# Lead ups by VectorE's lag, rows at an even pace, a selection put off and an earlier fetch of V, in a decoder layer on one core

## The chip, the cores and the metric

The kernel runs on one core of one Trainium2 chip. The metric is the time of the device in microseconds, of which the median over several runs is taken. TensorE (PE in the rows) does the matrix products, VectorE (DVE) elementwise work, searches and the gathered rows, ScalarE (ACT) activations and the emptying of PSUM, GpSimd (POOL) the indirect DMAs, SyncE (SP) the plain DMAs.

## The reference

One layer over 512 tokens of width 1024, float32. The cut below keeps what is computed.

```python
h = layer_norm(x, ln_emb_g, ln_emb_b)
rq, rk, rv, rg, fq, fk, fv, ff, gr, gf = jnp.split(h @ w_in[i], split_points, axis=-1)
y_ret = (silu(rg) * group_norm_heads(retention(rotary(rq), rotary(rk), rv))) @ w_ret_o[i]
y_fox = forgetting_attention(fq, fk, fv, log_sigmoid(ff + b_forget[i])) @ w_fox_o[i]
merged = sigmoid(gr + b0) * y_ret + sigmoid(gf + b1) * y_fox
h = layer_norm(ALPHA * h + merged @ w_out[i], ln1_g[i], ln1_b[i])
ple = sigmoid(h @ w_ple_gate[i] + b_ple_gate[i]) * (p[i] @ w_ple[i])
ch = peer(h, w_peer_q[i], peer_sub_keys[i], peer_u[i], peer_v[i]) + ple
h = layer_norm(ALPHA * h + ch, ln2_g[i], ln2_b[i])

def peer(x, ...):      # per token: 8 heads, 16 of 128*128 experts each
    sc = einsum(x @ w_q, sub_keys)            # two halves of 128 keys
    s, idx = top_k(sc, 16)                    # per half
    top_s, pos = top_k(all 256 sums, 16)      # the selection
    eid, gate = ids at pos, softmax(top_s)
    act = gelu(einsum(expert_u[eid], x)) * gate
    return einsum(act, expert_v[eid])
```

## The kernel before

The 512 tokens are four blocks of 128. Blocks 0 and 1 (`FIRST`) go ahead, blocks 2 and 3 (`REST`) follow, and the two pairs treat the experts differently.

For `FIRST`, each of the 128 (8 heads by 16) chosen experts of a token is fetched: one **row** is an indirect DMA on POOL (L1023) that brings 128 expert vectors, one for each token, 0.524 MB, and one VectorE instruction, either a product with the token summed (`row<-row,xg`, L1029, an up row, 256 of them) or an update of the sum (`h<-row,ghid,h`, L1039, a down row, 256). Eight buffers hold rows. For `REST` all 16384 experts are computed: 128 **banks** of 128 experts. The **up** of a bank is 8 matmuls of `h1f` with `ur` (a load of 1 MB holds two banks) into PSUM `hid` (two buffers), followed by a GELU on ScalarE into `a`. The down is 12 matmuls with V split in high and low parts (`vh`, `vl`). Between them the activation is multiplied with a dense gate `gw`, made by the **spread**.

The stages, by the profiled run: up to 24 us tokens are loaded, normalised and transposed; up to 300 `first_blocks` (projections and attention of `FIRST`); up to 410 `product_keys` of block 0 and of block 1, each by itself, and half of the embedding gate; up to 462 keys and values of `REST` (`keys_values`) and the start of its retention; up to 760 `last_blocks` (attention of `REST`, `w_out`, the norm, the other half of that gate); up to 906 `channel` begins with `product_keys` of `REST`, its embedding gate, in which `select` of block 2 runs; up to 1022 the spread of block 2, with `select` of block 3 beside it; up to 1130 the spread of block 3; up to 1182 remaining ups and the first loads of the dense loop; up to 1781 the dense loop over the banks; then the last norm and the output.

`lead` is 46: so many ups are done ahead of the dense loop (**lead ups**), and RES = 4 more into the accumulator's PSUM. A **spread** transposes the three routing tiles of a block (`gt`, copied by ScalarE to `gtr`), then makes, for each 8 tokens, two one-hot masks on VectorE (`oa`, `ob`), scales `oa` by the gate on ScalarE, multiplies the two on TensorE (`gp`) and copies the result on ScalarE to `stg` (two buffers). After each 32 tokens the full `stg` (2 MB) is written from ScalarE's queue to `gd` in DRAM, eight times in all; the dense loop reads it back as `gw`.

What sets the order: VectorE, POOL and TensorE run the instructions in the order in which the program emits them, from the product keys of `FIRST` on; a scheduler sets the order of ScalarE and SP. A `Feed` is a list of pieces of work with a rate; `tick()`, called after each group of a projection and each step of a spread, takes pieces: from `k.later`, from `k.side` (selections, norms), from `k.fill` (products of the embedding, later lead ups), then rows. Rows come from `k.feed` whenever `Clock.row()` allows. `Clock` adds up planned times of TensorE (`pe`), VectorE (`dve`) and the DMA (`dma`); a row is allowed when VectorE's plan, with this row, is not past TensorE's. Helper calls all record line L188 (L194 in the changed kernel).

Of the kernel before, what the change touches and what calls it, by code (L numbers as in the profile page):

```python
# [131 lines left out]
class Clock:  # L132
# [4 lines left out]
    def __init__(self):  # L137
        self.pe = self.dve = self.dma = 0.0
        self.before = None
# [23 lines left out]
    def row(self):  # L163

        if self.dve + self.ROW > self.pe or self.dma > self.pe + 5:
            return False
        self.dve = max(self.dve, self.pe - 12) + self.ROW
        self.dma = max(self.dma, self.pe - 5) + self.ROW
        return True
# [33 lines left out]
def setup(ctx, tc, I):  # L203
# [9 lines left out]
    k.feed, k.side, k.fill = Feed(), Feed(), Feed()  # L213
# [12 lines left out]
    def tick():  # L226
        due, k.later = k.later, []
        for f, *a in due:
            f(*a)
        k.side()  # L230
        k.fill()
        rows()
# [364 lines left out]
def attention(k, G, act, rq):  # L597
# [21 lines left out]
    side.drain()  # L619
    yf = slot([P, nt, 512], F32, "H4", k.uniq("yf"))  # L620
# [45 lines left out]
def first_blocks(k, unsplit):  # L666
# [4 lines left out]
    tokens_load(k, G)  # L671
    for t in G.blocks:
        tokens_norm(k, t)
        transpose_block(k, k.h0[:, t, :], act, t, 8)
# [15 lines left out]
    k.side.rate = k.fill.rate = 0.5  # L690
    k.fill.items = embeddings(k)
# [3 lines left out]
    k.fill.drain()  # L695
# [17 lines left out]
def last_blocks(k, act, rq, h10):  # L713
# [7 lines left out]
    k.h1 = k.slot([P, 8, G.N], F32, "S3", "h1f")  # L721
    for u, t in enumerate(G.blocks):
        layer_norm(k, k.h0[:, t, :], k.h0[:, t, :], g1, b1, st=sts[u], share=False)
# [47 lines left out]
def embeddings(k):  # L771
# [16 lines left out]
    return [(products, g, t) for g in range(2) for t in range(NT)]  # L788
# [104 lines left out]
def spread(k, sp, routed, n0, gd):  # L893
# [6 lines left out]
    nc.scalar.activation(tr, ps, AF.Copy)  # L900
    sh = [P, 8, P]
# [32 lines left out]
class Experts:  # L934


    def __init__(self, k, dense, gd, lead, ap, ph):
        self.k, self.gd, self.lead, self.ap, self.ph = k, gd, lead, ap, ph
        self.nd, self.ND = len(dense), len(dense) * P
        self.act, self.vw, self.gw = {}, {}, {}  # L940
# [14 lines left out]
    def load(self, b, dv):  # L955
        k, nc = self.k, self.k.nc
        if b % 2 == 0:
            self.vraw = dv.tile([P, 2, D], F32, tag="vraw", name=k.uniq("vr"))
            nc.sync.dma_start(self.vraw, k.I["vP"][b // 2])
        hi = dv.tile([P, D], F32R, tag="vhi", bufs=3, name=k.uniq("vh"))  # L960
        lo = dv.tile([P, D], F32R, tag="vlo", bufs=3, name=k.uniq("vl"))
        nc.scalar.activation(hi, self.vraw[:, b % 2], AF.Copy)
        self.vw[b] = (hi, lo, self.vraw[:, b % 2])
# [78 lines left out]
def channel(k, dense, lead, ctx):  # L1042
# [5 lines left out]
    ex = Experts(k, dense, gd, lead, ap, ph)  # L1048
    with ExitStack() as c1:
        k.pp = c1.enter_context(tc.tile_pool(name="pp2", bufs=4, space=PSUM))  # L1050
        k.px = c1.enter_context(tc.tile_pool(name="px2", bufs=2, space=PSUM))
        rp = c1.enter_context(tc.tile_pool(name="rp", bufs=2))
        routed = [[rp.tile([P, HEADS * K], F32, bufs=1, name=f"rt{n}_{i}") for i in range(3)] for n in range(2)]
        with ExitStack() as c2:
# [31 lines left out]
    nc.sync.dma_start(g2, bcast(I["ln2_g"], D))  # L1086
    nc.sync.dma_start(b2, bcast(I["ln2_b"], D))
# [7 lines left out]
    for b in range(2):  # L1095
        ex.load(b, dp)
# [4 lines left out]
    for b in range(3):  # L1101
        ex.gate(b, dp)
    for b in range(2):
        ex.remainder(*ex.act[b])
    done = lead + RES
    for b in range(NK):
        if b + 2 < NK:
            ex.load(b + 2, dp)
# [31 lines left out]
def decoder_layer(ctx, tc, I, lead):  # L1140
# [4 lines left out]
    with ExitStack() as c1:  # L1145
# [25 lines left out]
        k.side.rate = 1.25  # L1171
        k.clock.meet()
        for u, t in enumerate(FIRST.blocks):
# [3 lines left out]
            k.side.items += [g.route(rp, s16[:, 0], i16[:, 0]), (g.rows,)]  # L1177
        k.side.items += [(c2.close,)]
# [9 lines left out]
        last_blocks(k, act, rq, h1)  # L1188
    channel(k, list(REST.blocks), lead, ctx)
# [28 lines left out]
```

## Time and profile before

| | |
|---|---|
| median of three runs | 1838.2 us (1829.74 to 1840.3) |
| profiled execution, own time | 1832.67 us |
| its span | 1830.9 us |
| granted TensorE clock over the span | 0.964 |
| busy: TensorE, VectorE, ScalarE, POOL | 91%, 75%, 34%, 35% of the span |
| bytes moved by DMA | 566.51 MB, 309 GB/s over the span |

A row of a timeline gives the start, the duration, the engine, the line, the operation, what it writes and reads, and in brackets how long its engine had been idle and what ended that. One fp32 matmul leaves two records, so an up of 8 matmuls is x16. A table by stretch gives the busy time of each engine in it, the granted clock, the share of time in which the DMA engines were busy and what they moved.

### The profile page before, as it was taken

The page shows a single profiled execution, that of the slowest core. Times are in us where ns is not written, and L with a number is a line of the kernel's source. Part 1 is how long each engine was busy: PE and PEld are TensorE (multiplying, and loading weights), DVE is VectorE, ACT ScalarE, POOL GpSimd, SP SyncE. Part 2 cuts the span into 40 slices and gives each one's busy share as a digit, 9 for nine tenths or more (in the row PEclk, how much of TensorE's full clock was granted, in tenths as well). Part 3 has the DMA queues.
Part 4 walks back from the last instruction along what each step waited for, and adds up shares of the span by engine and source line. Part 5 has one row for each costly group of instructions (what it writes and reads, how often), then busy time and mean ns, then how long its engine had stood idle before and what let it go on. Part 6 is the DMA issues. An engine that isn't in the chain of part 4 may idle for free.

```text
span 1830.9 us, 23147 instructions
## 1 busy us (share of the span) xinstructions
PE 1666.7 (91%) x8224; PEld 1370.6 (75%) x8224; DVE 1375.3 (75%) x2624; ACT 614.6 (34%) x1160; POOL 648.9 (35%) x523
## 2 busy tenths in 40 slices
PE   5999999997899998899488989799999999999996
PEld 4898998873757885486377878588888887888785
DVE  6544364799778878889978775487878877887887
ACT  4445643212023320111355654233323333333332
POOL 1000000014567765432107352243434444544440
PEclk9999999999999999999789989899999999999998
DMA  7543455778899999995349999899999999999992
GB/s 264 167 138 127 146 163 191 249 237 323 309 341 403 409 409 407 364 376 204 124 132 369 305 398 312 314 408 383 389 391 406 402 371 373 410 408 393 402 367 91
DMA packets 171684, 566.51 MB, mean 309 GB/s; under 512 B 18352, under 2 KB 51632, under 8 KB 155184
## 3 DMA queue, kind: packets, MB, share of 16 engines
q1 hardware_dynamic: 64944, 279.78, 40.8%
q0 software_dynamic: 73728, 268.47, 37.9%
q10 hardware_dynamic: 32896, 16.78, 3.1%
q8 instruction: 65, 1.06, 0.2%
q14 instruction: 51, 0.42, 0.1%
HBM read 543.99 MB, written 20.97 MB: 309 GB/s over the span
## 4 chain that ended last, share of the span: by engine, by line
PE 47%; issue 20%; DVE 16%; DMA 14%; ACT 2%; POOL 1%; SPq 0%; DVEq 0%; POOLq 0%; ACTq 0%
PE hid L188 19%; PE acc L188 18%; PE pj L188 6%; DMA gd<-stg 5%; DMA row<-in_peer_v,geu 4%; DMA row<-in_peer_u,geu 3%; DVE h L1039 2%; PE gp L188 2%; DVE s L188 2%; DVE i L188 2%; DVE row L1029 1%; DVE w L188 1%; DVE pos L188 1%; DMA wr<-in_w_peer_q 1%; PE lg L188 1%
## 5 line engine op out<-in xcount | busy, mean ns | idle before, releaser
L1023 POOL DMA_INDIRECT row<-in_peer_v,geu x256 | 323.4, 1263 | 428.5 <-DVE h L1039 374.5
L1023 POOL DMA_INDIRECT row<-in_peer_u,geu x256 | 313.9, 1226 | 409.1 <-DVE row L1029 231.7
L188 PE MATMUL hid<-h1f,ur 128*128 128x256 f32 x1984 | 451.6, 381 | 3.1 <-DMA ur<-in_uT 2.6
L188 PEld LDWEIGHTS hid<-h1f,ur 128*128 128x128 f32 x1984 | 376.5, 191 | 57.2 <-issue 3.9
L1039 DVE SCALAR_TENSOR_TENSOR h<-row,ghid,h 128x1024 f32<-128x1024 f32 x256 | 327.5, 1279 | 22.1 <-DMA row<-in_peer_v,geu 19.4
L1029 DVE SCALAR_TENSOR_TENSOR row<-row,xg 128x1024 f32<-128x1024 f32 x256 | 306.8, 1217 | 19.4 <-DMA row<-in_peer_u,geu 18.9
L188 DVE TENSOR_TENSOR vl<-vr,vh 128x1024 fp32r<-128x1024 f32 x128 | 156.8, 1226 | 133.9 <-ACT vh L188 116.1
L188 PE MATMUL acc<-vh,ah 128*128 128x512 f32 x512 | 214.9, 420 | 0.0
L188 PE MATMUL acc<-vh,al 128*128 128x512 f32 x512 | 201.8, 394 | 11.8 <-DVE al L188 11.8
L188 PE MATMUL acc<-vl,ah 128*128 128x512 f32 x512 | 201.0, 393 | 4.8 <-DVE vl L188 4.8
L188 DVE TENSOR_TENSOR wl<-wr,wh 128x1024 fp32r<-128x1024 f32 x72 | 90.5, 1257 | 92.7 <-ACT wh L188 92.5
L188 ACT ACTIVATE vh<-vr 128x1024 fp32r<-128x1024 f32 x128 | 130.4, 1050 | 41.0 <-PE acc L188 27.0
L188 PE MATMUL pj<-h1f,wr 128*128 128x128 f32 (+1 forms) x768 | 124.0, 322 | 16.9 <-DMA wr<-in_w_peer_q 11.3
L188 ACT ACTIVATE a<-hid 128x256 f32<-128x256 f32 x124 | 47.1, 382 | 254.3 <-PE hid L188 254.3
L188 PEld LDWEIGHTS pj<-h1f,wr 128*128 128x128 f32 x768 | 111.7, 198 | 27.8 <-DMA wr<-in_w_peer_q 10.4
L188 PEld LDWEIGHTS acc<-vh,al 128*128 128x128 f32 x512 | 96.6, 189 | 35.9 <-DVE al L188 15.7
L188 ACT ACTIVATE ah<-a 128x256 fp32r<-128x256 f32 x128 | 53.1, 416 | 199.3 <-DVE a L188 178.2
L188 PE MATMUL pj<-hT,wr 128*128 128x256 f32 x512 | 117.6, 385 | 0.7 <-DMA wr<-in_w_in 0.7
L188 PEld LDWEIGHTS acc<-vl,ah 128*128 128x128 f32 x512 | 96.8, 189 | 26.4 <-DVE vl L188 5.5
L285 POOL TENSOR_TENSOR h<-h,b 128x512 f32<-128x512 f32 x6 | 9.7, 1619 | 294.9 <-ACT h L188 294.9
L188 PEld LDWEIGHTS acc<-vh,ah 128*128 128x128 f32 x512 | 96.7, 189 | 19.1
L188 PEld LDWEIGHTS pj<-hT,wr 128*128 128x128 f32 x512 | 97.4, 193 | 15.0 <-DMA wr<-in_w_in 1.1
(225 smaller groups left out, 2506.0 us busy)
## 6 DMA issues: line engine op xcount, KB each, us to landing
ur<-in_uT SPq DMA_DIRECT2D x64, 1024.0 KB, 8.3
vr<-in_vP SPq DMA_DIRECT2D x64, 1024.0 KB, 8.5
wr<-in_w_in SPq DMA_DIRECT2D x104, 512.0 KB, 4.0
wr<-in_w_peer_q SPq DMA_DIRECT2D x48, 512.0 KB, 4.6
gd<-stg ACTq DMA_DIRECT2D x8, 2048.0 KB, 25.7
gw<-gd SPq DMA_DIRECT2D x32, 512.0 KB, 9.4
wr<-in_w_ret_o SPq DMA_DIRECT2D x16, 512.0 KB, 5.7
wr<-in_w_out SPq DMA_DIRECT2D x16, 512.0 KB, 5.9
```

The costliest lines, as they stand in the source:

```text
L188: return f(*a, **kw)
L285: nc.gpsimd.tensor_tensor(dst[:, sl], dst[:, sl], b[:, sl], op=ALU.add)
L1023: k.tc.nc.gpsimd.indirect_dma_start(out=r, out_offset=None, in_=src, in_offset=bass.IndirectOffsetOnAxis(ap=self.e[:, c:c + 1], axis=0))
L1029: self.k.tc.nc.vector.scalar_tensor_tensor(r, r, 1.0, self.x, op0=ALU.mult, op1=ALU.mult, accum_out=self.hid[:, c:c + 1])
L1039: self.k.tc.nc.vector.scalar_tensor_tensor(h1, r, self.hid[:, c:c + 1], h1, op0=ALU.mult, op1=ALU.add)
```

## The change

- `Clock.row()` allows a row only if the planned DMA is at most 2 us past TensorE (5 before). Once `pace` is set, 3.4 us of TensorE's plan, a row is due every 3.4 us, with up to 8 held over, whatever VectorE's plan says. `pace` is set after the output projection of `REST`.
- A new feed `k.slow` takes the selection and the rows of block 1. Its rate is 0 until the projection of `fv` in the attention of `REST`, then 0.8. The selection of block 0 stays in `k.side`, at rate 2 (1.25 before).
- The products of the embedding (`pw`) are emitted at once at the start of `first_blocks`, ahead of the tokens' norms and transposes, and so are their loads.
- The lead ups are in `k.fill` from the start of `channel`, at up to 8 a tick, as long as the plan of VectorE is over 2 us past the pace of TensorE's (`clock.pe`) and more than RES are left. Before, some were emitted ahead of the first spread by the same test, and the rest evenly over the spreads. The selection of block 2 runs at rate 2.25, without a condition (2, only with VectorE free).
- The transposes of the routing are a function of their own, `by_slot`, with `k.fill()` ahead of it. Before the second spread the routing pool is closed and V's loads for banks 0 to 3 are issued (2 of 1 MB). The loads of `g2`, `b2` come after the first gates.

```diff
     def row(self):
-        if self.dve + self.ROW > self.pe or self.dma > self.pe + 5:
+        if self.dma > self.pe + 2:
+            return False
+        if self.pace:
+            if self.due > self.pe:
+                return False
+            self.due = max(self.due, self.pe - 8 * self.pace) + self.pace
+        elif self.dve + self.ROW > self.pe:
             return False
...
         k.side()
+        k.slow()
         k.fill()
         rows()
...
     side.drain()
+    k.slow.rate = 0.8
     yf = slot([P, nt, 512], F32, "H4", k.uniq("yf"))
...
     tokens_load(k, G)
+    embeddings(k)
     for t in G.blocks:
...
-    k.side.rate = k.fill.rate = 0.5
-    k.fill.items = embeddings(k)
+    k.side.rate = 0.5
...
     k.h1 = k.slot([P, 8, G.N], F32, "S3", "h1f")
+    k.clock.pace = 3.4
...
-    return [(products, g, t) for g in range(2) for t in range(NT)]
+    for g in range(2):
+        for t in range(NT):
+            products(g, t)
...
+    def fetch(self, b, dv):
+        v = dv.tile([P, 2, D], F32, tag="vraw", name=self.k.uniq("vr"))
+        self.k.nc.sync.dma_start(v, self.k.I["vP"][b // 2])
+        self.vraw[b], self.vraw[b + 1] = v[:, 0], v[:, 1]
...
+    k.fill.items, k.fill.rate = [(ex.up, b) for b in range(lead)], 8
+    k.fill.when = lambda: len(k.fill.items) > RES and k.clock.dve > k.clock.pe + 2
...
-            k.side.items, k.side.rate = [select(k, rp, s16[:, 0], i16[:, 0], *routed[0])], 2
-            k.side.when = k.clock.free
+            k.side.items, k.side.rate = [select(k, rp, s16[:, 0], i16[:, 0], *routed[0])], 2.25
...
-            k.fill.items = [(ex.up, b) for b in range(lead)]
-            while k.clock.dve > k.clock.pe + 2:
-                k.fill.step()
-            k.fill.rate = (len(k.fill.items) - RES) / 64
             for n in range(len(dense)):
-                for _ in spread(k, sp, routed[n], n * P, gd):
+                k.fill()
+                tr = by_slot(k, sp, routed[n])
+                if n == len(dense) - 1:
+                    c0.close()
+                    dv = ctx.enter_context(tc.tile_pool(name="dv", bufs=2, side="right"))
+                    for b in (0, 2):
+                        ex.fetch(b, dv)
+                for _ in spread(k, sp, tr, n * P, gd):
                     k.tick()
...
-        k.side.rate = 1.25
...
-            k.side.items += [g.route(rp, s16[:, 0], i16[:, 0]), (g.rows,)]
-        k.side.items += [(c2.close,)]
+            feed = k.slow if u else k.side
+            feed.items, feed.rate = [g.route(rp, s16[:, 0], i16[:, 0]), (g.rows,)], 0 if u else 2
...
         last_blocks(k, act, rq, h1)
+        k.slow.drain()
+        c2.close()
```

On TensorE, at its start: `tr` are the transposes of the tokens, `pj` the projections, `pw` the embedding products. Before:

```order
L188 MATMUL tr_120<-ident,h_65 128x128 x4
L188 MATMUL tr_127<-ident,h_65 128x128 x4
L188 MATMUL tr_154<-ident,h_65 128x128 x4
L188 MATMUL tr_161<-ident,h_65 128x128 x4
L188 MATMUL pj_201<-h0h,wh_205 128x256
```

And now:

```order
L194 MATMUL pw_106<-pwH_102,pwH_101 128x512 x2
L194 MATMUL pw_112<-pwH_102,pwH_101 128x512 x2
L194 MATMUL pw_118<-pwH_102,pwH_101 128x512 x2
L194 MATMUL pw_124<-pwH_102,pwH_101 128x512 x2
L194 MATMUL pw_131<-pwH_103,pwH_101 128x512 x2
L194 MATMUL pw_137<-pwH_103,pwH_101 128x512 x2
L194 MATMUL pw_143<-pwH_103,pwH_101 128x512 x2
L194 MATMUL pw_149<-pwH_103,pwH_101 128x512 x2
L194 MATMUL tr_175<-ident,h_65 128x128 x4
```

The eight pairs of products moved from between the projections to the head.

On TensorE, at the transposes of block 2's routing (`gt`), with the last products of the embedding gate (`pj`) ahead and the mask products (`gp`) and lead ups (`hid`) around. Before:

```order
L188 MATMUL pj_6247<-wr_6292,h1f 128x512
L188 MATMUL pj_6248<-wr_6292,h1f 128x512
L188 MATMUL hid_6403<-h1f,ur_6401 128x256 x8
L188 MATMUL hid_6414<-h1f,ur_6401 128x256 x8
L188 MATMUL hid_6427<-h1f,ur_6425 128x256 x8
L188 MATMUL hid_6438<-h1f,ur_6425 128x256 x8
L188 MATMUL hid_6451<-h1f,ur_6449 128x256 x8
L188 MATMUL gt_6462<-ident,rt_0_5644 128x128
L188 MATMUL gt_6462<-ident,rt_1_5645 128x128
L188 MATMUL gt_6462<-ident,rt_2_5646 128x128
L188 MATMUL gp_6475<-oa_6468,ob 128x128 x4
```

And now:

```order
L194 MATMUL pj_6430<-wr_6528,h1f 128x512
L194 MATMUL pj_6431<-wr_6528,h1f 128x512
L194 MATMUL hid_6571<-h1f,ur_6569 128x256 x8
L194 MATMUL hid_6582<-h1f,ur_6569 128x256 x8
L194 MATMUL gt_6593<-ident,rt_0_5638 128x128
L194 MATMUL gt_6593<-ident,rt_1_5639 128x128
L194 MATMUL gt_6593<-ident,rt_2_5640 128x128
L194 MATMUL gp_6615<-oa_6599,ob 128x128 x4
L194 MATMUL hid_6627<-h1f,ur_6625 128x256 x8
L194 MATMUL hid_6638<-h1f,ur_6625 128x256 x8
```

Of the lead ups ahead of `gt`, two stand directly before it and twelve further up, between the groups of the key projections and of the gate; before, all five stood here.

On VectorE, at the first masks: the end of block 2's selection (`rt_2`), the masks, the selection of block 3 (`iff`, `cand`). Before:

```order
L188 TENSOR_TENSOR rt_2_5646<-rt_2_5646,gsm_6389 128x128
L188 TENSOR_TENSOR oa_6468<-iota,gtr_6466 128x1024
L188 TENSOR_TENSOR ob<-iota,gtr_6466 128x1024
L188 TENSOR_TENSOR oa_6471<-iota,gtr_6466 128x1024
L188 TENSOR_TENSOR ob<-iota,gtr_6466 128x1024
L188 CAST iff_6485<-i_1103_5657 128x256
L188 TENSOR_TENSOR cand_6487<-s_1102_5656 128x8x64
```

And now:

```order
L194 TENSOR_TENSOR rt_2_5640<-rt_2_5640,gsm_6557 128x128
L1059 SCALAR_TENSOR_TENSOR h_65<-row_6600,ghid_2841,h_65 128x1024
L1059 SCALAR_TENSOR_TENSOR h_65<-row_6603,ghid_2841,h_65 128x1024
L1059 SCALAR_TENSOR_TENSOR h_65<-row_6606,ghid_2841,h_65 128x1024
L194 TENSOR_TENSOR oa_6599<-iota,gtr_6597 128x1024
L194 TENSOR_TENSOR ob<-iota,gtr_6597 128x1024
L194 TENSOR_TENSOR oa_6611<-iota,gtr_6597 128x1024
L194 TENSOR_TENSOR ob<-iota,gtr_6597 128x1024
```

Three down rows now stand ahead of the first masks, where before the masks followed the selection at once.

## Rows read from the trace of the kernel before

**Rows 1.** The page's slices, 40 of 45.8 us: TensorE's busy tenths, GB/s moved.
```profile
PE   5999999997899998899488989799999999999996
...
GB/s 264 167 138 127 146 163 191 249 237 323 309 341 403 409 409 407 364 376 204 124 132 369 305 398 312 314 408 383 389 391 406 402 371 373 410 408 393 402 367 91
```
**Rows 2.** By stretch: us; busy PE, PEld, DVE, ACT, POOL; clock, DMA share, GB/s.
```profile
410.00:462.00 52.00, 36.70 (x103) 19.04 (x103) 50.04 (x139) 9.80 (x14) 23.95 (x19) 0.94 0.88 328
...
462.00:760.00 298.00, 282.22 (x1190) 201.76 (x1190) 236.85 (x402) 64.21 (x117) 193.51 (x155) 0.98 0.98 376
...
760.00:906.00 146.00, 114.67 (x467) 86.31 (x467) 128.00 (x409) 22.97 (x36) 44.70 (x38) 0.89 0.72 271
906.00:1022.00 116.00, 97.79 (x543) 89.00 (x544) 94.02 (x157) 67.93 (x183) 40.95 (x27) 0.89 0.67 240
1022.00:1130.00 108.00, 96.43 (x554) 87.78 (x553) 84.65 (x92) 63.01 (x180) 50.26 (x33) 0.94 0.96 346
1130.00:1182.00 52.00, 38.80 (x160) 32.57 (x159) 12.87 (x27) 10.61 (x20) 8.76 (x9) 0.84 0.93 350
1182.00:1781.00 599.00, 587.90 (x2634) 495.68 (x2633) 487.54 (x687) 187.87 (x312) 267.56 (x225) 1.00 0.98 389
```
**Rows 3.** TensorE's timeline at the start.
```profile
10.46 1.12 PE L188 MATMUL tr<-ident,h 128*128 128x128 f32 x4 [10.46 <-DVE h L188]
...
24.34 0.41 PE L188 MATMUL pj<-h0h,wh 128*128 128x256 f32 x1
...
29.63 0.28 PE L188 MATMUL pj<-h0h,wl 128*128 128x256 f32 x1
...
31.89 1.88 PE L188 MATMUL pw<-pwH,pwH 128*128 128x512 f32 x4
```
**Rows 4.** TensorE's timeline, 410 to 462: what ended its waits.
```profile
417.13 14.00 PE L188 MATMUL pj<-wr,hT 128*128 128x512 f32 x32 [3.55 <-DVE sg L188]
...
461.89 0.77 PE L188 MATMUL rs<-rq,rk 128*128 128x128 f32 x2 [9.80 <-DVE sm L188]
```
**Rows 5.** TensorE's timeline, 780 to 1182.
```profile
780.81 8.69 PE L188 MATMUL pj<-h1f,wr 128*128 128x256 f32 x32 [6.45 <-DMA wr<-in_w_peer_q]
...
898.09 0.45 PE L188 MATMUL gt<-ident,rt 128*128 128x128 f32 x1 [14.34 <-DVE m L188]
...
1004.13 3.78 PE L188 MATMUL gp<-oa,ob 128*128 128x128 f32 x16 [6.78 <-ACT oa L188]
...
1018.92 3.62 PE L188 MATMUL hid<-h1f,ur 128*128 128x256 f32 x16
1022.38 0.49 PE L188 MATMUL gt<-ident,rt 128*128 128x128 f32 x3
...
1086.95 2.08 PE L188 MATMUL gp<-oa,ob 128*128 128x128 f32 x8 [8.50 <-ACT oa L188]
...
1129.19 10.53 PE L188 MATMUL hid<-h1f,ur 128*128 128x256 f32 x48
...
1169.57 8.87 PE L188 MATMUL acc<-h1f,ur 128*128 128x256 f32 x32 [5.46 <-DMA ur<-in_uT]
```
**Rows 6.** VectorE's timeline: six down rows, and the first mask.
```profile
807.11 7.87 DVE L1039 SCALAR_TENSOR_TENSOR h<-row,ghid,h 128x1024 f32<-128x1024 f32 x6
...
905.73 1.22 DVE L188 TENSOR_TENSOR oa<-iota,gtr 128x1024 f32<-128x1024 f32 x1 [1.15 <-ACT gtr L188]
```
**Rows 7.** ScalarE's timeline: a wait in block 2's selection; eight scalings of `oa`.
```profile
863.15 1.06 ACT L188 ACTIVATE w<-iff 128x1024 f32<-128x1024 f32 x1 [15.29 <-DVE iff L188]
...
944.83 2.44 ACT L188 ACTIVATE oa<-oa,gtr 128x128 f32<-128x128 f32 x8
```
**Rows 8.** Groups, 1022 to 1130: busy us, mean ns, idle before, its releasers.
```profile
L188 ACT ACTIVATE stg<-gp 128x512 f32<-128x512 f32 x32 | 18.7, 591 | 20.5 <-DMA gd<-stg 12.2 <-PE gp L188 8.2
```
**Rows 9.** The view of `stg`: its eight writes to `gd`, issue to landing.
```profile
DMA to landing us min/median/max: 13.5/25.7/38.4
```
**Rows 10.** TensorE's waits in the dense loop: us in total, times, longest.
```profile
PE acc L188 <- DVE al L188: 11.1, 11, 1.0
```

More of the change, by code (lines that the diff above doesn't have):

```diff
@@ L138, in __init__ @@
         self.pe = self.dve = self.dma = 0.0
-        self.before = None
+        self.before, self.pace, self.due = None, None, 0.0
     def matmul(self, a, kw):
@@ L212, in setup @@
     k.n = 0
-    k.feed, k.side, k.fill = Feed(), Feed(), Feed()
+    k.feed, k.side, k.slow, k.fill = Feed(), Feed(), Feed(), Feed()
     k.later = []
@@ L694, in first_blocks @@
     k.side.drain()
-    k.fill.drain()
     m = attention(k, G, act, rq)
@@ L890, with by_slot @@
 SG = 32
-def spread(k, sp, routed, n0, gd):
+def by_slot(k, sp, routed):
     nc = k.nc
@@ L900, in spread @@
     nc.scalar.activation(tr, ps, AF.Copy)
+    return tr
+def spread(k, sp, tr, n0, gd):
+    nc = k.nc
     sh = [P, 8, P]
@@ L939, in __init__ @@
         self.nd, self.ND = len(dense), len(dense) * P
-        self.act, self.vw, self.gw = {}, {}, {}
+        self.act, self.vw, self.gw, self.vraw = {}, {}, {}, {}
     def up(self, b, ps=None):
@@ L953, in up, with load @@
         self.act[b] = a
-    def load(self, b, dv):
-        k, nc = self.k, self.k.nc
[L957 to L963, printed above, removed]
+    def fetch(self, b, dv):
+        v = dv.tile([P, 2, D], F32, tag="vraw", name=self.k.uniq("vr"))
+        self.k.nc.sync.dma_start(v, self.k.I["vP"][b // 2])
+        self.vraw[b], self.vraw[b + 1] = v[:, 0], v[:, 1]
+    def load(self, b, dp, dv):
+        k, nc = self.k, self.k.nc
+        if b not in self.vraw:
+            self.fetch(b, dv)
+        hi = dp.tile([P, D], F32R, tag="vhi", bufs=3, name=k.uniq("vh"))
+        lo = dp.tile([P, D], F32R, tag="vlo", bufs=3, name=k.uniq("vl"))
+        nc.scalar.activation(hi, self.vraw[b], AF.Copy)
+        self.vw[b] = (hi, lo, self.vraw[b])
     def gate(self, b, dp):
@@ L1048, in channel @@
     ex = Experts(k, dense, gd, lead, ap, ph)
+    k.fill.items, k.fill.rate = [(ex.up, b) for b in range(lead)], 8
+    k.fill.when = lambda: len(k.fill.items) > RES and k.clock.dve > k.clock.pe + 2
+    c0 = ExitStack()
     with ExitStack() as c1:
@@ L1051, in channel @@
         k.px = c1.enter_context(tc.tile_pool(name="px2", bufs=2, space=PSUM))
-        rp = c1.enter_context(tc.tile_pool(name="rp", bufs=2))
+        rp = c0.enter_context(tc.tile_pool(name="rp", bufs=2, side="right"))
         routed = [[rp.tile([P, HEADS * K], F32, bufs=1, name=f"rt{n}_{i}") for i in range(3)] for n in range(2)]
@@ L1085, in channel @@
     g2, b2 = gb[:, 0, :], gb[:, 1, :]
-    nc.sync.dma_start(g2, bcast(I["ln2_g"], D))
-    nc.sync.dma_start(b2, bcast(I["ln2_b"], D))
     def finish(t):
@@ L1095, in channel @@
     for b in range(2):
-        ex.load(b, dp)
+        ex.load(b, dp, dv)
     for i in range(RES):
@@ L1102, in channel @@
         ex.gate(b, dp)
+    nc.sync.dma_start(g2, bcast(I["ln2_g"], D))
+    nc.sync.dma_start(b2, bcast(I["ln2_b"], D))
     for b in range(2):
@@ L1107, in channel @@
         if b + 2 < NK:
-            ex.load(b + 2, dp)
+            ex.load(b + 2, dp, dv)
         while done < NK and done < lead + RES + (NK - lead - RES) * (b + 1) / (NK - 6):
```

## The prediction

> **What bounds the kernel now.** I read the page's slices first [rows 1]: TensorE is nearly full except at the start, around slice 10 (410 to 460 us) and in slices 20 to 26 (870 to 1190 us), at the start of which what the DMA engines move drops too, from some 400 GB/s to 124. Then a table of busy time by stretch [rows 2]. In the dense loop (1182 to 1781) TensorE is busy 587.9 of 599 us at full clock and the DMA engines 0.98 of the time at 389 GB/s: nothing to gain there but fewer bytes. From 760 to 1182 TensorE's sum is 347.7 of 422 us, at a granted clock of 0.84 to 0.94, so 74 us are idle; from 410 to 462 it is 36.7 of 52. These are the places that the change touches, with the 24 us ahead of the first projection. Last I read the timelines there for which wait ends last. At the start TensorE waits 10.46 us for the first normalised token block, then in short steps until the projections run (the matmul at 24.34 is one of the first of some 40) [rows 3]. At 410 to 462 it waits 3.55 us and 9.80 us for VectorE [rows 4]. From 760 on [rows 5] it waits for a weight (6.45 us), for VectorE's selection of block 2 (14.34), and in the spreads for `oa` scaled by ScalarE (6.78, 8.50); after them for `ur` (5.46, and others like it).
>
> All sums are made against the profiled execution (own time 1832.7 us, span 1830.9); the median of the runs is 5.5 us above, and I add that at the end. About 0.5% is what a measurement of this kernel can tell from no change.
>
> **A, the embedding products at the start.** They are 8 products of two matmuls. Before, they stand between the projections (4 records in 1.88 us from 31.89, so 32 records make about 14.4 us) [rows 3]. After, they stand ahead of the first transposes. So 14.4 us of TensorE work leaves the projections and lies in a wait. Against this: `pT` and two tiles of `w_ple` (1.57 MB) go ahead of `w_in` on SP's queue, in a slice that moves 264 GB/s [rows 1], so some 6 us; and the products' copies on ScalarE share the three `px` buffers with the transposes behind them. Before, TensorE came to its full clock at 29.63 us (a matmul's time falls from 0.41 to 0.28 us there [rows 3]), after some 7 us of projections at about half the rate, so that their work effectively starts at 25.5. I take the projections to begin at 36 after, warmed by the products: 36 - 25.5 - 14.4 = -4 us. If the products finish early it is -8; if `w_in` is late by another 9 us, +5.
>
> **B, block 0's selection quicker, block 1's later (300 to 462).** VectorE's sum of instruction times from the first product-key search to the first decay product of REST's retention falls from 132.4 to 124.9 us by the order and the durations of the trace: part of a selection leaves, but 35 gathered rows stand there instead of 19, at 1.31 us each (6 in 7.87 us) [rows 6]. VectorE is the one that TensorE waits for here (50.04 busy of 52) [rows 2, 4], so up to 13.35 us of waits could shrink, and I take -7. What is late next is the DMA: in the last 45 us, 27 rows are 14.1 MB and the weights 6.3 MB, 453 GB/s, above the 410 of the fullest slice [rows 1], so the rows set the pace for part of it and the gain could be nothing. Ends 0 and -14. Block 1's selection then runs among REST's attention, where VectorE was busy 236.85 of 298 us [rows 2]. It has room there, and the rows displaced are those that were put earlier: 0.
>
> **C, lead ups and rows around the spreads (760 to 1182).** By the order, the lead ups ahead of the transposes of block 2's routing are 14 instead of 5, in the first spread 17 instead of 18, in the second 9 instead of 18, then 6 instead of 5. One is 3.46 us (from 1018.92 to the next row, 1022.38) [rows 5]. VectorE has 36 rows instead of 20 from the first search of REST to the first mask.
> - Up to the first mask: VectorE decides (128.0 of 146 us busy [rows 2]); 16 rows by 1.31 is 21 us more. The 6.45 us for `wr` should go, as `ur` no longer waits on another engine ahead of it on SP's queue. So the first mask comes at about 921, not 905.7: +15 (from +8 to +21). TensorE's 114.7 us and 9 more ups of 3.46 make 146 in 161: they fit, if they start when the order has them.
> - First spread, 905.7 to 1022.4, 116.7 us: after, VectorE's sum is 99 us as before (16 pairs of masks at 1.22 each half [rows 6], 27 rows, the selection, now interleaved), TensorE's the 97.8 of the stretch less one up, 94, and ScalarE's the 67.9 [rows 2]. I take VectorE's and 5 us of start: 104, so -13 (from -18 to 0).
> - Second spread, 1022.4 to 1129.3, 107 us: TensorE's work falls from 96.4 [rows 2] by nine ups to 65 us; VectorE's is 16 pairs of masks and 18 rows, 63. What is late next is the write of `stg`: two buffers, each filled in four steps of ScalarE of 2.44 us of scaling [rows 7] and two copies of 0.59 [rows 8], 14.6 us, and landing 25.7 us after its issue at the median [rows 9]. Two buffers in turn make (25.7 + 14.6)/2 = 20 us for one write, 80 for four: -27. With landings of 13.5 us [rows 9] TensorE decides, 65 (-42); with all at 38.4 it is 26.5 us and 106 (-1).
> - 1129.3 to 1182, 53 us: 1 up more, but V's two first pairs are there already, and the loads of `ur` that TensorE waited for come sooner: 46, so -6 (from -15 to +3).
>
> Sum: +15 - 13 - 27 - 6 = -31 (ends -48 and +8, as the extremes do not fall together).
>
> **D, the dense loop.** 12 more rows (246, not 234) of 0.524 MB are 6.3 MB, less 2 MB of V: 4.3 MB on 233 MB takes 389 GB/s to 396, where 410 is the most that a slice moved [rows 1]. VectorE gets 15 us more on 487.5 of 599. TensorE's waits there are 11.1 us for `al` [rows 10], which could double: +2, ends 0 and +11.
>
> **A page against the trace.** The spread's writes and the gathered rows go from different queues, and from 906 to 1022 the DMA engines are 0.67 busy, from 1022 to 1130 0.96 [rows 2]; the landings spread from 13.5 to 38.4 us [rows 9]. The Trainium skill, "DMA: Bandwidth & Descriptors", section "Queues, rings and completion order", says that each DMA engine takes turns between the queue rows it has work for, a packet at a time. By that rule a write of `stg` is stretched by whatever else is queued, and an even flow of rows beside both spreads speaks against this change. The trace agrees in that its landings differ by nearly three times; that the rows are the reason, no row shows.
>
> **The sum.** -4 - 7 - 31 + 2 = -40: 1793 against the own time, 1798 against the median. Its own range is 1783 to 1812, from the nearer ends of B and C.
>
> **The rivals.**
> - *The writes set the second spread.* It keeps nearly its old length: landings stay long, 25 to 27 us a write, because rows now run beside the first spread's writes too. For it: two waits of 6.78 and 8.50 us there already end in a chain from the buffers [rows 5], and the share of the DMA is 0.96 [rows 2]. Against: these waits are 17 of 107 us. C is then -6: 1832.7 - 4 - 7 - 6 + 2 + 5.5 = 1823.
> - *It does not do what it says.* The early ups stand on TensorE, in order, behind two `hid` buffers that ScalarE has to empty, and ScalarE's queue waits there on VectorE: 15.29 us at the selection of block 2 [rows 7], the time of four ups. Then TensorE gets to 14 ups only by standing still, product keys and gate come later, and the first mask with them; the 31 us gained in the second spread are spent before it. 1835.
> - *Slower: DMA full throughout.* If rows, `u` and the writes at once find no spare transfer, from 906 on, writes land in 38 us or more: a write takes 28 us, both spreads keep their 224 us, and with 15 us for the later first mask and -7 behind, C is +8; B gains nothing, D takes its +11, A -4: +15, so 1832.7 + 15 + 5.5 = about 1853. It decides from a mean landing of some 38 us. For it: 0.96 to 0.98 busy in three stretches [rows 2]. Against: from 760 to 1022 there is a third of the DMA free, and total bytes are unchanged.
> - *Better still*: landings of 15 us and all of B, below 1783.
>
> **How the numbers follow.** Forecast (1783 to 1812) 0.52; below it 0.09; writes 1823 (1812 to 1831) 0.20; no effect 1835 (1828 to 1845) 0.10; slower 1853 (above 1842) 0.09. The range takes the forecast, the writes and most of no effect, and half of the better: 1778 to 1838. Half a per cent is 9 us: faster means under 1829. That is 0.52 + 0.09 + 0.16 = 0.77; within, the rest of the writes and most of no effect, 0.15; slower 0.08.
>
> **What would show it.** A: the first projection near 36 us, with no `pw` behind it. B: the waits for `sg` and `sm` before 462 together under 7 us. C: hid work between the product-key groups, with no idle time ended by ScalarE ahead of it; the first mask near 921; the second spread near 80 us; landings near 25. D: dense loop within 3 us of 599. It is wrong if `hid` waits for ScalarE early, if landings stay over 35 us, or if the dense loop starts after 1175.

## The result and the profile after

| | before | changed |
|---|---|---|
| median | 1835.5 us (8 runs, 1829.7 to 1840.3) | 1821.8 us (8 runs, 1818.3 to 1829.6) |
| ratio | | 0.9926, 95% interval 0.9905 to 0.9948 |
| profiled execution, own time / span | 1832.7 / 1830.9 us | 1824.6 / 1822.9 us |

The change makes the kernel faster by 0.74%, 14 us, where 40 were forecast. The two profiled executions are 8 us apart, and what is added up below adds up to these 8. The table by stretch of the changed kernel, against [rows 2] (us; busy PE, PEld, DVE, ACT, POOL; granted clock, share of the DMA, GB/s):

```profile
410.00:462.00 52.00, 38.49 (x110) 19.82 (x108) 41.88 (x70) 5.98 (x10) 39.55 (x31) 0.94 1.03 409
...
760.00:906.00 146.00, 122.50 (x544) 99.82 (x543) 115.61 (x366) 19.91 (x35) 49.16 (x44) 0.93 0.83 304
906.00:1022.00 116.00, 99.37 (x519) 84.50 (x518) 105.58 (x192) 62.87 (x160) 46.44 (x31) 0.93 0.81 274
1022.00:1130.00 108.00, 93.48 (x553) 85.02 (x551) 76.95 (x84) 75.00 (x211) 27.06 (x19) 0.95 0.94 308
1130.00:1182.00 52.00, 43.39 (x171) 36.11 (x170) 22.92 (x41) 14.45 (x25) 10.41 (x10) 0.87 0.68 257
1182.00:1781.00 599.00, 585.73 (x2620) 492.88 (x2619) 497.55 (x704) 187.32 (x311) 281.51 (x233) 1.00 1.00 397
```

From 410 to 462 VectorE, full before, is now busy 41.88 of 52 us, and the DMA is at its ceiling instead (409 GB/s, not 328). The dense loop moves 397 GB/s, not 389. To see where the time went, one follows the same instruction of TensorE through both traces; the lead is the time by which the changed kernel is ahead:

| instruction of TensorE | before, us | changed, us | lead |
|---|---|---|---|
| first product key of `FIRST` | 309.2 | 305.2 | 4.0 |
| retention of `REST`, behind the first decay product | 461.9 | 463.8 | -1.9 |
| first attention scores of `REST` | 538.6 | 543.0 | -4.4 |
| end of the transposes of `h1f` | 758.0 | 760.7 | -2.7 |
| first product key of `REST` | 760.7 | 773.3 | -12.6 |
| first mask product, block 2 | 908.3 | 942.8 | -34.5 |
| transposes of block 3's routing | 1022.4 | 1042.5 | -20.1 |
| end of the last mask product | 1129.3 | 1116.5 | 12.8 |
| first down product | 1181.5 | 1169.2 | 12.4 |
| end of the span | 1830.9 | 1822.9 | 8.0 |

A second trace of the changed order (e7_V_late below) reaches these marks 3 to 9 us earlier, from 302.1 us at the first to 1813.7 at the last. A single lead is no surer than that; where several kernels share the order of a stretch, its length is compared over all of them below.

Two stretches lose what was to be a gain: 305 to 540, and 760 to 943. The rows of TensorE's timeline that answer to [rows 3 to 5], with the wait ahead of each in brackets:

```profile
35.24 0.59 PE L194 MATMUL pj<-h0h,wh 128*128 128x256 f32 x2 [0.86 <-ACT h0h L194]
...
463.81 0.77 PE L194 MATMUL rs<-rq,rk 128*128 128x128 f32 x2 [13.66 <-DVE sm L194]
...
773.29 12.03 PE L194 MATMUL pj<-h1f,wr 128*128 128x256 f32 x48 [12.62 <-DMA wr<-in_w_peer_q]
796.20 9.08 PE L194 MATMUL pj<-h1f,wr 128*128 128x256 f32 x32 [10.88 <-DMA wr<-in_w_peer_q]
...
935.05 0.48 PE L194 MATMUL gt<-ident,rt 128*128 128x128 f32 x1 [8.56 <-DVE rt L194]
...
942.77 2.04 PE L194 MATMUL gp<-oa,ob 128*128 128x128 f32 x8 [5.76 <-ACT oa L194]
...
1135.64 10.02 PE L194 MATMUL hid<-h1f,ur 128*128 128x256 f32 x32 [5.28 <-ACT a L194]
```

The wait for `sm` grew from 9.80 to 13.66 us, and the wait for the weights of `REST`'s product keys from 6.45 to 23.5 in two pieces.

VectorE, ahead of that `sm` (start, duration, instruction, in brackets what it waited for), shows what filled the time: rows, many of them waiting for their DMA.

```profile
443.40 1.23 DVE L1049 SCALAR_TENSOR_TENSOR row<-row,xg 128x1024 f32<-128x1024 f32 x1 [0.68 <-DMA row<-in_peer_u,geu]
...
445.32 1.23 DVE L1049 SCALAR_TENSOR_TENSOR row<-row,xg 128x1024 f32<-128x1024 f32 x1 [0.69 <-DMA row<-in_peer_u,geu]
...
447.79 1.22 DVE L1049 SCALAR_TENSOR_TENSOR row<-row,xg 128x1024 f32<-128x1024 f32 x1 [1.24 <-DMA row<-in_peer_u,geu]
```

These come 1.9 and 2.5 us apart, not 1.31. Up to that `sm`, thirteen of the 35 rows waited so, 9.7 us in all (time, times, longest); in the kernel before none did.

```profile
DVE row L1049 <- DMA row<-in_peer_u,geu: 9.7, 13, 1.3
```

At 766 the reason for the late weights can be read. SyncE issues the first keys and weights of `REST` the moment that VectorE ends the last sum of the embedding gate; first VectorE's row, then SyncE's:

```profile
765.89 0.69 DVE L194 TENSOR_TENSOR h<-h,sg 128x512 f32<-128x512 f32 x1
```
```profile
766.65 0.33 SPq L194 DMA_DIRECT2D keys<-in_keysT  x1
767.03 1.56 SPq L194 DMA_DIRECT2D wr<-in_w_peer_q  x3
```

In the kernel before, the same two loads went 14 us earlier, and `ur` was what came behind that sum:

```profile
752.53 0.33 SPq L188 DMA_DIRECT2D keys<-in_keysT  x1
752.91 1.37 SPq L188 DMA_DIRECT2D wr<-in_w_peer_q  x3
...
763.11 0.93 SPq L188 DMA_DIRECT2D ur<-in_uT  x2
```

The diff has the cause in a line that looks like bookkeeping:

```diff
-        rp = c1.enter_context(tc.tile_pool(name="rp", bufs=2))
+        rp = c0.enter_context(tc.tile_pool(name="rp", bufs=2, side="right"))
```

The routing pool `rp` went to the right side of the memory, so the pools opened after it slid down. The weights' buffers stood at bytes 152640 to 164928 of a partition, over the pool `tp`, free when the norm is done; now they stand at 130688 to 142976, over `q1`, which the embedding gate still uses.

### The profile page after: what moved, and what is told of

Read it like the earlier page. It is cut to its first block, busy times and chain, and to the rows that moved or that the text cites. A ratio compares the mean times of both kernels' runs of the same rounds, so it can differ in the third digit from the quotient of the medians.

```text
span 1822.9 us, 23135 instructions
## 1 busy us (share of the span) xinstructions
PE 1668.6 (92%) x8224; PEld 1367.2 (75%) x8224; DVE 1369.3 (75%) x2624; ACT 616.5 (34%) x1163; POOL 642.4 (35%) x523
## 4 chain that ended last, share of the span: by engine, by line
PE 55%; issue 18%; DVE 15%; DMA 8%; ACT 2%; POOL 1%; SPq 1%; ACTq 0%; DVEq 0%; POOLq 0%
PE hid L194 18%; PE acc L194 18%; PE pj L194 13%; DVE h L1059 4%; DMA wr<-in_w_peer_q 2%; DMA row<-in_peer_u,geu 2%; PE lg L194 2%; PE gp L194 1%; DVE ob L194 1%; DVE h L194 1%; DVE oa L194 1%; DVE row L1049 1%; DVE s L194 1%; POOL row L1043 1%; DVE pos L194 1%
## 5 line engine op out<-in xcount | busy, mean ns | idle before, releaser
L1043 POOL DMA_INDIRECT row<-in_peer_u,geu x256 | 309.2, 1208 | 444.4 <-DVE row L1049 258.2
```

What stands on the lines that cost most here:

```text
L1043: k.tc.nc.gpsimd.indirect_dma_start(out=r, out_offset=None, in_=src, in_offset=bass.IndirectOffsetOnAxis(ap=self.e[:, c:c + 1], axis=0))
```

## The experiments

Each ratio is against the kernel before on the same chip, so it is to be compared with 0.9926; 0.001 is 1.8 us. All kernels but e11 start from the changed one.

**e1_weights**: the work tiles of that stage are put over `q1`, the weights and keys over `tp` (`Halves` hands tiles called keys to the pool `kk`, all others to `work`).

```diff
-            k.wp = c2.enter_context(tc.tile_pool(name="wp2", bufs=3))
-            kp = c2.enter_context(tc.tile_pool(name="kp", bufs=2))
+            work = c2.enter_context(tc.tile_pool(name="kp", bufs=2))
+            k.wp = c2.enter_context(tc.tile_pool(name="wp2", bufs=3))
+            kp = Halves(c2.enter_context(tc.tile_pool(name="kk", bufs=2)), work)
```

> The changed kernel with one edit in channel(): the pools are opened in another order, so that the weights and keys of REST's product keys lie over memory that is free once the norm has run, and the work tiles lie over q1's memory instead; the order on TensorE, VectorE and GpSimd is the changed kernel's. Theory M (memory): in the changed kernel these loads are issued at 766.65, right after the embedding gate's last sum ends at 766.58, since they lie over that stage's tiles. Then here they are issued some 11 to 14 us earlier, TensorE's wait of 12.62 us for wr shrinks below 4, the one of 10.88 may stay, and the time falls by 8 to 16 us, to 1806 to 1814. Theory D (the DMA is full): rows and weights share a full DMA at 760 to 800, so earlier issues land no earlier in sum; the two waits together stay near 20 us and the time within 4 us of 1822.

Measured: 1811.6 us, ratio 0.9891 (0.9855 to 0.9927). SyncE's row, and TensorE's:

```profile
754.46 0.33 SPq L205 DMA_DIRECT2D keys<-in_keysT  x1
```
```profile
763.49 12.05 PE L205 MATMUL pj<-h1f,wr 128*128 128x256 f32 x48 [2.87 <-ACT sg L205]
787.39 8.61 PE L205 MATMUL pj<-h1f,wr 128*128 128x256 f32 x32 [11.85 <-DMA wr<-in_w_peer_q]
```

The loads go 12 us earlier, the first wait is gone (the 2.87 us left are for ScalarE), the second stays, and all later marks come 9 to 12 us earlier (first mask product 933.5, first down product 1157.6). The ratio alone would not tell: its interval overlaps that of the changed kernel. The stretch does: from the end of the transposes of `h1f` to the first mask product, five kernels with the changed pools take 181.5 to 184.2 us (changed, e2, e3, e7, e9), and three with these pools 171.8 to 173.7 (e1, e5, e12). The memory is the cause of the first wait, and it costs some 10 us.

**e2_selections**: block 1's selection back in the side feed, with block 0's, at rate 1.25.

```diff
-            feed = k.slow if u else k.side
-            feed.items, feed.rate = [g.route(rp, s16[:, 0], i16[:, 0]), (g.rows,)], 0 if u else 2
+            k.side.items += [g.route(rp, s16[:, 0], i16[:, 0]), (g.rows,)]
+        k.side.items += [(c2.close,)]
```

> The changed kernel with the selections put back: block 0's and block 1's both in the side feed at rate 1.25 ahead of REST's attention, as before; the rest of the change stays. Theory R (rows): in the changed kernel 14 more rows that the DMA brings at 410 GB/s stand ahead of the decay product that TensorE waits for 13.66 us, so putting the selection off lost some 10 us between 305 and 540. Then here the wait falls back to about 9.8 us, the attention begins 6 to 10 us earlier, and the time falls by 4 to 10 us, to 1812 to 1818, unless the selection's later rows are missed in the dense loop. Theory S: the selection put off is a gain of some 7 us that another thing hides; then the time rises to 1826 to 1832.

Measured: 1811.9 us, ratio 0.9873 (0.9847 to 0.9898). The wait for `sm` is 8.18 us, the attention's first scores come at 534.7 (543.0), the transposes of `h1f` end at 749.9 (760.7). By the order 19 rows stand ahead of `sm` again, and 16 more in the attention; from there to the dense loop all counts are those of the changed kernel. So this part of the change costs some 10 us. Whether by the rows or by the place of the selection, the next kernel tells.

**e9_rows_held**: the selection stays put off, only the rows pause.

```diff
+        k.clock.dma = k.clock.pe + 20
         keys_values(k, REST, act, rk, rv)
```

> The changed kernel with one added line: ahead of REST's keys and values the planner's DMA time is set 20 us past TensorE's, so that rows pause. By the order 19 rows instead of 35 stand ahead of the decay product of the retention, as in the kernel before; block 1's selection stays put off, and all later places keep their rows, so that the dense loop gets 16 rows more (262). Theory R (the rows, at the DMA's limit, delay the decay product): TensorE's wait there falls from 13.66 us to under 6, REST's attention begins 8 to 12 us earlier, and the dense loop takes 16 x 0.6 = 10 us back: 1818 to 1824. Theory S (the wait is another thing's, and putting the selection off costs by itself): the wait stays over 10 us, the attention begins within 3 us of the changed kernel's, and the time rises to 1828 to 1834.

Measured: 1813.3 us, ratio 0.9919 (0.9889 to 0.9949). TensorE's wait for `sm` is gone altogether, and the stretch that had 15 us idle is full, at full clock:

```profile
410.00:462.00 52.00, 50.99 (x173) 31.34 (x172) 34.75 (x75) 7.52 (x14) 28.73 (x22) 1.00 0.96 368
```

The attention's first scores come at 518.9, 24 us ahead of the changed kernel and 20 ahead of the kernel before. It was the rows that cost the changed kernel its time, and not the selection put off: e2 has the same 19 rows ahead of `sm`, but the selections in their old place, and waits:

```profile
458.52 0.77 PE L194 MATMUL rs<-rq,rk 128*128 128x128 f32 x2 [8.18 <-DVE sm L194]
```

From the first product key of `FIRST` to the end of the transposes of `h1f`, seven kernels with the changed order of this stretch take 452.3 to 455.5 us (changed, e1, e3, e4, e6, e7, e8), two with the order of before 448.4 and 448.8 (before, e11), three with the selections back 445.6 to 445.9 (e2, e5, e10), and e9 takes 431.5. In the total the ratio shows no gain, within its interval: the dense loop has 262 rows instead of 246 and takes 654.5 us from its first to its last down product, not 641.7.

**e3_embedding**: the embedding products back among the projections (`k.fill.items = embeddings(k)` at rate 0.5).

> The changed kernel with the embedding products back among the projections. The traces have the changed kernel 4.0 us ahead at the first product keys (305.2 against 309.2), which I put down to this part alone: the time then rises by 4 us, to 1826. Rival: the lead comes from other parts or is lost later in the wait for the decay product; then it stays within 2 us of 1822.

Measured: 1824.9 us, ratio 0.9940 (0.9917 to 0.9964). The first product key comes at 310.3, 5.1 us later. The ratio agrees with a loss of 3 us but can't tell it from none, and one pair of traces can't either. Over all traces it is 4 us: with the products at the head this mark stands at 302.1 to 307.8 us in eleven kernels (mean 304.8), with them among the projections at 306.8 to 310.3 in three (before, e3, e11; mean 308.8).

**e4_even_ups**: the lead ups at their even rate from the spreads on.

```diff
-    k.fill.items, k.fill.rate = [(ex.up, b) for b in range(lead)], 8
-    k.fill.when = lambda: len(k.fill.items) > RES and k.clock.dve > k.clock.pe + 2
...
+            k.fill.items = [(ex.up, b) for b in range(lead)]
+            while k.clock.dve > k.clock.pe + 2:
+                k.fill.step()
+            k.fill.rate = (len(k.fill.items) - RES) / 64
```

> The changed kernel with the lead ups at their even rate from the spreads on, as before (5, 18, 18 instead of 14, 17, 9); pace of rows, early V and selections stay. Theory U: the ups put ahead of the first mask shorten the second spread by some 30 us and cost some 17 at the first mask, so without them the time rises by 10 to 18 us, to 1832 to 1840. Rival: the even pace of rows is what shortens the second spread, and the ups only move; then the time stays within 4 us of 1822.

Measured: 1827.6 us, ratio 0.9968 (0.9952 to 0.9984), 8 us worse than the changed kernel. The first mask product is at 926.9 (942.8), but the second spread takes 97 us (74) and ends at 1118.3, so the ups only move time ahead of the dense loop. The loss arises in the loop, 650.4 us with 244 rows instead of 641.7 with 246. Of that 2.4 us are the last norm of block 1, which VectorE runs near the loop's end: it stands one step earlier here, and TensorE waits 6.88 us for the `al` behind it, not 4.51 for a `vl`. Its other waits in the loop are 3.2 us longer too (18.2, not 15.0). The rest I can't derive.

**e6_no_pace**: `k.clock.pace = 3.4` left out.

> The changed kernel without the pace of rows: rows go by VectorE's plan alone, as before, with the tighter limit on the DMA. By the order 240 rows stand ahead of the dense loop instead of 266, ups are 12, 13 and 21 around the routing's transposes. Theory: the pace keeps rows beside the spreads where the DMA has room, so without it 26 more rows (13.6 MB, 33 us of a DMA at 410 GB/s) fall into a dense loop whose DMA is full: the spreads get some 25 us shorter in sum, the dense loop 20 to 35 longer, the time 1820 to 1835. Rival: the dense loop has room for them; then the time falls to 1800 to 1810.

Measured: 1838.4 us, ratio 1.0039 (1.0025 to 1.0053). Second spread and dense loop:

```profile
1022.00:1130.00 108.00, 89.84 (x497) 78.84 (x497) 50.96 (x51) 66.73 (x188) 9.71 (x9) 0.95 0.78 263
1182.00:1781.00 599.00, 577.04 (x2554) 482.08 (x2552) 518.43 (x738) 183.91 (x305) 332.83 (x255) 0.99 1.02 410
```

VectorE and the DMA have room in the spread (51 of 108 us, 263 GB/s), and the loop with 272 rows is at 410 GB/s and takes 657.4 us. The first down product is at 1169.8, as in the changed kernel, so these two traces show no delay there from the 26 rows that the pace puts ahead of the loop. The ups move as well, by their own rule (12, 13 and 21 of them, not 14, 17 and 15): with this rule, the pace is worth 20 us.

**e11_pace_alone**: the kernel before with the new `row()` and the pace, nothing else.

> The kernel before with the pace of rows alone (3.4 us, and the tighter limit on the DMA); no other part of the change. Taking the pace out of the changed kernel cost 17 us, so if the parts add up this kernel is 14 to 18 us under the kernel before, which was 1831 to 1835 here. Rival: the pace is worth something only together with the lead ups put ahead, which give VectorE the time for the rows; by the order 268 rows stand ahead of the dense loop, against 278 in the kernel before, so the dense loop gets 10 more rows, 4 to 7 us, and the time is that of the kernel before or 5 us above.

Measured: 1831.0 us, ratio 1.0009 (0.9982 to 1.0036). Nothing: the rival holds. The pace without the rule for the ups gains nothing here; in the changed kernel, taking out either loses, 8 us (e4) and 20 us (e6). A kernel with these two rules and nothing else was not run, so that they alone carry the change is not shown.

**e7_V_late**: `ex.fetch` ahead of the second spread left out.

> The changed kernel with V's first two pairs fetched with the first loads of the dense loop, as before. Theory: the early fetch takes 2 MB (5 us at 410 GB/s) off the stretch from the last mask product to the first down product, so that without it the first down product comes 3 to 8 us later and the time is 1825 to 1830. Rival: that stretch waits for ScalarE and for ur, not for V; then the time stays within 3 us of 1822.

Measured: 1820.0 us, ratio 0.9947 (0.9926 to 0.9967). This is no test: the scheduler of SyncE's queue issues the two loads in the spread as before, since their pool is there:

```profile
1036.80 0.80 SPq L194 DMA_DIRECT2D vr<-in_vP  x2
```

It is the changed kernel once more (there they go at 1043.28), and shows how far two profiled executions of one order differ: its first down product is at 1160.7, not 1169.2.

**e8_hold**: as e1, and no row due for 24 us at the start of `REST`'s product keys (`k.clock.due = k.clock.pe + 24`).

> As e1_weights, and no row is due for the first 24 us of planned TensorE time of REST's product keys: by the order 1 row stands between the embedding gate's last sum and the first search, instead of 14, and the dense loop has 14 more. Theory: the second wait (11.85 us in e1_weights) is rows and weights sharing a full DMA; then it shrinks below 5 us, the spreads come 6 to 10 us earlier, the dense loop takes some back (14 rows are 7.3 MB, up to 18 us at 410 GB/s), and the time is 1804 to 1818. Rival: the wait is the two loads of ur (2 MB) ahead of the weights on the same queue, not rows; then the wait stays over 8 us and the time rises above 1815.

Measured: 1817.0 us, ratio 0.9928 (0.9903 to 0.9954). The second wait falls only by half:

```profile
778.53 8.67 PE L205 MATMUL pj<-h1f,wr 128*128 128x256 f32 x32 [6.23 <-DMA wr<-in_w_peer_q]
```

So rows are half of that wait. What the other half is stays open: two loads of `ur`, the rival on record, stand ahead of these weights on SyncE's queue here too, and no kernel tests them. The first mask product is 10 us ahead of e1's, 4 of them already at the end of the transposes, and the dense loop, with 260 rows, 11 us longer (651.8).

**e5_both**: e1 and e2 in one.

> The changed kernel with both edits that gained: the pools in the other order (weights of REST's product keys over memory that is free early) and both selections in the side feed ahead of REST's attention. If the two costs are separate (one at 410 to 540 us, one at 760), the gains add up: 10 + 10 under the changed kernel's 1821.8, so 1800 to 1804. Rival: both shift the same thing, the burst of rows at the weights (the wait of 9.4 to 11.9 us that both runs still show at the second group of weights); then earlier loads meet more rows, and the time stays at 1808 to 1812.

Measured: 1805.6 us, ratio 0.9865 (0.9843 to 0.9887): by the ratio hardly better than e2 (0.9873). The sum of the two gains would be 0.9838, just outside the interval, but e1's and e2's own ratios are no surer, so a shortfall is likely and not shown. The second group of weights waits 6.67 us still.

**e10_pace_3**: e5 with a pace of 3.0 us.

> e5_both (both repairs) with a row due every 3.0 us instead of 3.4. By the order 281 rows stand ahead of the dense loop instead of 266. If a row that is left to the dense loop costs about 0.6 us there (three kernels so far: 234, 246 and 272 rows in the loop, 637.4, 641.7 and 657.4 us from its first to its last down product) and the stretch of the spreads still has room on the DMA, the time falls by 5 to 9 us, to 1797 to 1801. Rival: the spreads are full by now, VectorE's 15 more rows (20 us) and the writes of stg push them back by as much; then it stays within 3 us of 1805 or rises.

Measured: 1807.2 us, ratio 0.9861 (0.9830 to 0.9893), the rival's. The dense loop has 231 rows and 637.6 us (642.1 in e5), but the first down product comes 7.9 us later.

**e12_weights_rows**: e1, and the pause of e9 with 14 us instead of 20.

> Both repairs in the changed kernel, with its selections as they are: the pools of e1_weights, and rows paused ahead of REST's keys and values (14 us of planned DMA), so that 24 rows stand ahead of the retention's decay product, not 35, and 255 ahead of the dense loop, not 266. From e9_rows_held (the wait of 13.66 us gone, the attention 24 us earlier, the dense loop 12.8 longer with 16 more rows) and e1_weights (10 us): the decay product's wait is under 4 us, the attention begins 14 to 22 us earlier, the first group of weights no longer waits, the dense loop takes 8 to 10 back, and the time is 1798 to 1806. Rival: the DMA is the limit of the whole, so that what is gained ahead comes back as rows and weights meet later; then it is 1808 to 1814, as with either repair alone.

Measured: 1797.1 us, ratio 0.9797 (0.9757 to 0.9836), 2.0% below the kernel before and the best of all. Stretch and waits, the last the sum in the dense loop and ahead of it (us, times, longest):

```profile
410.00:462.00 52.00, 50.75 (x171) 31.18 (x171) 41.18 (x80) 7.61 (x14) 35.65 (x28) 1.00 1.03 408
```
```profile
761.98 6.35 PE L205 MATMUL pj<-h1f,wr 128*128 128x256 f32 x16 [7.03 <-DMA wr<-in_w_peer_q]
```
```profile
PE acc L205 <- DVE al L205: 24.3, 19, 6.9
```

The DMA is at its ceiling there too, but 24 rows instead of 35 leave the decay product in time. The first down product is at 1137.3, 32 us ahead of the changed kernel, and the loop with 257 rows takes 649.7 us, 8 longer.

## Why the prediction was wrong

Faster was right, and the size was three times too large. That 1821.8 lies in the range is owed to the range's width, which takes in two of the rivals; the forecast's own range, 1783 to 1812, was missed. Step by step, against the profiled pair (-4 + 6.7 - 15 + 4.3 = -8):

- **A** (-4): right in size. The first projection is at 35.24 us, 36 forecast; the lead at the first product keys is 4.0 us, and 4 as the mean over all traces (e3). "Warmed by the products" did not come about: under the products, up to 29 us, and under the transposes the granted clock was 1.00, from 35.0 to 38.6 us it was 0.57, near the lower of its two levels (1.2 GHz), and 1.00 again from 39 us. The first projections took 0.41 us a matmul, as before, though for some 3.5 us instead of 7.

```profile
38.48 0.41 PE L194 MATMUL pj<-h0l,wh 128*128 128x256 f32 x1
...
39.04 0.28 PE L194 MATMUL pj<-h0l,wh 128*128 128x256 f32 x1
```

- **B** (-7): wrong in sign; the lead goes from 4.0 to -2.7, so +6.7, and over all traces of either order the loss is 4 to 7 us (e9). The step that failed is the price of a row, "1.31 us each", VectorE's own time, and the end of the range at 0. I had seen that 453 GB/s were asked of a DMA that gives 410, and took this as a bound on the gain. But rows stand in order ahead of the decay product on VectorE: a row that the DMA delays delays `sm` with it, and that has no bound at zero. VectorE's sum did fall, but it now waits 9.7 us for rows, which it did not before. e9 shows the rows as the cause. The premise of B, that putting block 1's selection off frees VectorE, held: before, VectorE worked up to `sm` on 19 rows and that selection, waiting for no row, and with 19 rows and the selection put off (e9) the stretch is 17 us shorter than before. What was let into the freed time, 16 rows more, cost more than that.
- **C** (-31): -15 from the end of `h1f`'s transposes to the first down product. The step that failed is "the 6.45 us for `wr` should go, as `ur` no longer waits on another engine ahead of it on SP's queue". The order said that `ur` waits for nothing; it also showed that the keys wait for VectorE, in both kernels, and I did not ask for which instruction. It had become the gate's last sum. The two waits went from 9.2 (with the 2.78 ahead of 760.74) to 23.5 us, 14 us. e1 shows the memory for the first wait alone; the second, where the 6.45 us were to go, is 10.88 us here, 11.85 in e1 and 6.23 in e8, so it was not removed in any of them. Behind the waits stand the 31 us of the nine more ups, of which the prediction says "they fit, if they start when the order has them"; e4, with five of these ups instead of fourteen, has the first mask product 16 us earlier, so behind the late weights they did not. In sum the first mask came at 940.2, not 921, and the part up to the first mask product took 32 us more than before, not 15.
- The spreads themselves were nearly right: 102.4 us from the first mask to block 3's transposes (104 forecast), 74 for the second (80).
- From the last mask product to the first down product 46 was forecast and 52.7 measured. V is there early, but ScalarE's copy of it stands ahead of the GELUs of the last lead ups, and waits 8.50 us for the last write of `stg`, over whose pool it lies:

```profile
1132.37 2.95 ACT L194 ACTIVATE vh<-vr 128x1024 fp32r<-128x1024 f32 x3 [8.50 <-DMA gd<-stg]
```

  TensorE's 5.28 us ahead of 1135.64 come from that. I had no kernel that undoes it.
- **D** (+2): the loop takes 641.7 us from first to last down product, not 637.4, so +4.3, inside its ends; waits for `al` rise from 11.8 to 15.0.
- **The rivals.** "The writes set the second spread" gave 1823, near what was measured, by a mechanism that did not occur: ScalarE waited for a write of `stg` 2.0 us in all, not 26.1, and landings were 17.8 to 20.0 us at the median in the four kernels with these spreads whose traces have them (e5, e7, e8, e9), not 25.7 [rows 9]. "Does not do what it says" fell too: TensorE runs from 805 to 926 us without a wait, so ScalarE's queue did not hold the ups. "DMA full throughout" was right in its resource, and wrong in its place: not the writes but the rows ahead of `sm`, and the dense loop.
- The rule of the Trainium skill, "DMA: Bandwidth & Descriptors", section "Queues, rings and completion order", that an engine takes turns between its queues, would have the writes stretched by rows beside them. The traces agree in order: with 60 rows issued on POOL from the first to the last mask product (before, 27 and 33) the median landing is 25.7 us, with 39 to 45 (e5, e7, e8, e9) 17.8 to 20.0, and with 8 (e6) 12.6. What was wrong is that an even flow of rows "speaks against this change": rows stood beside both spreads before it too, and the changed kernel has fewer there, 27 and 14. That the rows alone make the difference no run shows, since the ups beside the spreads, and with them the loads of `ur`, differ as well.

What stays open: the other half of the second wait for weights, and why the dense loop of e4 and e11 is 6 to 9 us longer than that of the changed kernel with two rows fewer in it. TensorE's waits in the loop (25.1 and 24.1 us, not 19.5) are 5 to 6 of it.

## What to carry to other kernels

A row of work that needs both an engine and a transfer is priced by the slower of the two where it stands, and if it stands in order ahead of something that another engine waits for, the excess is paid there; a limit on the DMA bounds a gain on neither side of zero. When a diff moves a pool, look at whose memory each first load now lies over and when that is last read, before counting instructions. Two rules, of which one moves work and the other fills the hole that it leaves, are to be judged together: taking either out of the changed kernel lost time, and the pace added alone to the kernel before gained none. Before one trusts a difference of a few us between two traces, one looks for a second trace of the same order.

## What was not expected of the hardware

A row left to the dense loop costs about half of its transfer, as an estimate from twelve kernels, which differ in more than their rows. First to last down product, by the rows in the loop: 231 rows 637.6 us (e10), 234 637.4 (before), 246 639.7 to 642.1 (changed, e1, e2, e3, e5, e7), 257 649.7 (e12), 260 651.8 (e8), 262 654.5 (e9), 272 657.4 (e6): 20 us for 41 rows, 0.5 us each, where 0.524 MB at 410 GB/s are 1.28. Two kernels with 244 rows, e11 with 647.8 and e4 with 650.4, lie off this line; their longest wait for `al`, 6.9 us near the end, stands in e9 and e12 too. No slice of the two pages moved more than 414 GB/s.
